# A two-layer decoder trunk: weight pieces of the next projection set between the transpose groups of the attention turn, and the value products moved to a transpose bank

## The chip, the core and the metric

The kernel runs on one core of a Trainium2 chip. The metric is the device time of one execution in microseconds, and the times below are medians over the runs of the kernel before.

## The reference

Two layers of a decoder trunk work on 512 tokens of width 2048 in float32. The first layer is a mixer of gated recurrence and spatial gating with one input and one output projection; the change doesn't touch it. The second layer is multi-head latent attention with 16 heads, and the change lies in it:

```
z = h @ w_in
cq, ckv, kpe, gate = split_sizes(z, [C_Q_RANK, C_KV_RANK, C_ROPE, C_WIDTH])
q = (rms_norm(cq, q_norm) @ w_qb).reshape(bsz, T, C_HEADS, C_QK)
kv = (rms_norm(ckv, kv_norm) @ w_kvb).reshape(bsz, T, C_HEADS, C_NOPE + C_V)
...
s = jnp.einsum('bqhd,bkhd->bhqk', q_blk.astype(jnp.float32), kf) * scale
s = jnp.where(k_idx[None, :] <= q_idx[:, None], s, neg)
p = jax.nn.softmax(s, axis=-1)
return jnp.einsum('bhqk,bkhv->bqhv', p.astype(v.dtype), v)
...
return (o * jax.nn.silu(gate)) @ w_out
```

Ranks are 512, a head has 128 plain and 64 rotary query columns (C_QK is 192) and 128 value columns.

## The kernel before

Each float32 factor of a projection is split into a high and a low part that TensorE takes at full rate, and each product is three matmuls (high x high, high x low, low x high). `feat_steps` (L214 to L216) has the weights as the stationary operand, `tok_steps` (L209 to L211) the activations. Weights come as a plan of pieces of 128 x 1024 or fewer elements. `piece(n)` hands out piece n and starts the load of the pieces up to n + 3: a DMA into a ring of three `raw` tiles, a cast to `whi` on ScalarE (L168, or L177 for a piece cut in two column sets) and a subtraction to `wlo` on VectorE (L169, L178), in rings of four. `split_into` (L279 on ScalarE, L280 on VectorE) makes the two parts of any other tile, and so empties a PSUM bank.

The eight PSUM banks are three rings: `mm` of four, `sc` of two, `tp` of two. A tile that is asked for takes the place of the oldest of its ring, whose readers must be done.

The attention goes by pairs of heads. For pair p there are `proj_q` (36 matmuls in two pieces into three banks, then the rotation L761 to L765 and the splits), `proj_k` (24 matmuls into two banks) and `proj_v` (24 matmuls of 256 columns for each of two banks). A turn of head h is made of four functions. `att_transpose(h)` turns the probabilities of h in three groups (L900: four, four and two 128 x 128 transposes, each into a `tp` bank, each split into PT tiles). `att_scores(h + 1)` makes the scores of the next head by 20 matmuls (L878 to L882) into two `sc` banks and one `mm` bank, and then its softmax: causal mask and row maximum (L885), its negative (L888), the exponential on ScalarE (L889), reciprocal and scaling (L891, L892), in row blocks 3, 2, 0, 1. `att_values(h)` multiplies values by probabilities (L911 to L913, 12 matmuls) into a third `sc` tile, which L914 multiplies by the gate. Below, **turn A** is the turn of an even head, which runs beside the query projection of the next pair, and **turn B** that of an odd head, beside its key and value projections.

The functions are written in this order, and a scheduler then places each instruction in the queue of its engine by priority and estimated readiness; each queue runs in order. So the order on an engine can differ from the order of the calls: in turn A the third transpose group stands among the scores, and the value products stand behind the first matmuls of `proj_k`.

Of the kernel before, what the change touches and what calls it, by code (L numbers as in the profile page):

```python
# [10 lines left out]
F32 = mybir.dt.float32  # L11
# [7 lines left out]
P = 128  # L19
# [25 lines left out]
def trunk_kernel(ctx, tc, x, positions, norm_pre, norm_post, ev_w_in, ev_lb_logits, ev_a_onorm,  # L45
                 ev_b_ln_w, ev_b_ln_b, ev_b_ws, ev_b_bias, ev_w_out, od_w_in, od_q_norm, od_w_qb,
                 od_kv_norm, od_w_kvb, od_w_out, inv_freq, out, x1_dram):
    nc = tc.nc
# [3 lines left out]
    sm = ctx.enter_context(tc.tile_pool(name="sm", bufs=2))  # L52
# [4 lines left out]
    def mm_bank():  # L57
        return pmm.tile([P, 512], F32, name="mm", tag="mm")

    def sc_bank():  # L60
        return psc.tile([P, 512], F32, name="sc", tag="sc")

    def tp_bank():
        return ptp.tile([P, 512], F32, name="tp", tag="tp")
# [123 lines left out]
    def piece(n):  # L188
        issue_to(n + AHEAD)
        return ready.pop(n)  # L190
# [16 lines left out]
    def tok_steps(o, act, k, sl, wh, wl, first, last):  # L207
        hh, hl = act(k)
        nc.tensor.matmul(o, hh[:, sl], wh, start=first, stop=False, skip_group_check=True)  # L209
        nc.tensor.matmul(o, hh[:, sl], wl, start=False, stop=False, skip_group_check=True)  # L210
        nc.tensor.matmul(o, hl[:, sl], wh, start=False, stop=last, skip_group_check=True)  # L211

    def feat_steps(ps, hi, lo, hh, hl, first, last):
        nc.tensor.matmul(ps, hi, hh, start=first, stop=False)  # L214
        nc.tensor.matmul(ps, hi, hl, start=False, stop=False)  # L215
        nc.tensor.matmul(ps, lo, hh, start=False, stop=last)  # L216
# [61 lines left out]
    def split_into(dst_hi, dst_lo, src):  # L278
        nc.scalar.copy(dst_hi, src)  # L279
        nc.vector.tensor_tensor(dst_lo, src, dst_hi.bitcast(F32), ALU.subtract)  # L280
# [35 lines left out]
    pl = {}  # L316
# [440 lines left out]
    cq_act, ckv_act = c_act(0), c_act(8)  # L757
# [11 lines left out]
    stk, _ = piece(pl["kpe"])  # L769
# [37 lines left out]
    def q_of(h):  # L807
        u = 12 * ((h // 2) % 2) + 2 * (h % 2)
        return R[:, u, :], R[:, u + 1, :]

    def k_of(h):
        u = 12 * ((h // 2) % 2) + 4 + 2 * (h % 2)
        return R[:, u, :], R[:, u + 1, :]

    def v_of(p):
        u = 12 * (p % 2) + 8
        return (R[:, u:u + 2, :].rearrange("p a (i c) -> p (a i) c", c=256),
                R[:, u + 2:u + 4, :].rearrange("p a (i c) -> p (a i) c", c=256))

    def p_of(h):  # L820
        base = 3 * (h % 2)
        pb = G[:, base + 1, :]
        return {3: G[:, base, :], 2: pb[:, 0:384], 0: pb[:, 384:512], 1: G[:, base + 2, 0:256]}

    def proj_q(p):
        qps = [mm_bank() for _ in range(3)]
        for s in range(2):
            wh, wl = piece(pl["q", p] + s)
            for t in (2, 0, 1):
                ts = slice(t * P, (t + 1) * P)  # L830
                for kk in range(2):
                    k = 2 * s + kk
                    hh, hl = cq_act(k)
                    feat_steps(qps[t], wh[:, kk, ts], wl[:, kk, ts], hh, hl, k == 0, k == 3)
        rope_half(zr, qps[2], qps[2], sw, 128)
        for m in range(2):
            split_into(*q_of(2 * p + m), qps[m])
            own, oth = slice(64 * m, 64 * m + 64), slice(64 - 64 * m, 128 - 64 * m)
            qs_ = QS[(2 * p + m) % 4]
            nc.scalar.copy(qs_[own], zr[own])  # L840
            nc.vector.tensor_tensor(qs_[oth], zr[own], qs_[own].bitcast(F32), ALU.subtract)  # L841
# [3 lines left out]
    def proj_k(p):  # L845
        kps = [mm_bank() for _ in range(2)]
        kv_pieces[p] = [piece(pl["kv", p] + s) for s in range(2)]
        for m in range(2):
            ms = slice(m * 256, m * 256 + 128)
            for k in range(4):  # L850
                wh, wl = (w[:, k % 2] for w in kv_pieces[p][k // 2])
                hh, hl = ckv_act(k)
                feat_steps(kps[m], wh[:, ms], wl[:, ms], hh, hl, k == 0, k == 3)
            split_into(*k_of(2 * p + m), kps[m])

    def proj_v(p, a):
        Vh, Vl = v_of(p)
        vps = mm_bank()
        for i in range(2):
            sl = slice((2 * a + i) * P, (2 * a + i + 1) * P)  # L860
            for k in range(4):
                wh, wl = (w[:, k % 2].rearrange("p (a c) -> p a c", a=2)[:, :, 128:256]
                          for w in kv_pieces[p][k // 2])
                tok_steps(vps[:, i * 256:i * 256 + 256], ckv_act, k, sl, wh, wl, k == 0 and i == 0, k == 3)
        split_into(Vh[:, 2 * a:2 * a + 2, :].rearrange("p i c -> p (i c)"),
                   Vl[:, 2 * a:2 * a + 2, :].rearrange("p i c -> p (i c)"), vps)

    def att_scores(h):
        (Qh, Ql), (Kh, Kl), qs_, pv = q_of(h), k_of(h), QS[h % 4], p_of(h)
        mx = sm.tile([P, 4], F32, name="mx")  # L870
        nm = sm.tile([P, 4], F32, name="nm")
        su = sm.tile([P, 4], F32, name="su")
        sa, sb, sc = sc_bank(), sc_bank(), mm_bank()
        sp = {3: sa, 2: sb[:, 0:384], 0: sb[:, 384:512], 1: sc[:, 0:256]}
        for j in (3, 2, 0, 1):
            n, o = (j + 1) * P, sp[j]
            qs = slice(j * P, (j + 1) * P)
            nc.tensor.matmul(o, Qh[:, qs], Kh[:, 0:n], start=True, stop=False)  # L878
            nc.tensor.matmul(o, Qh[:, qs], Kl[:, 0:n], start=False, stop=False)
            nc.tensor.matmul(o, Ql[:, qs], Kh[:, 0:n], start=False, stop=False)  # L880
            nc.tensor.matmul(o, qs_[:, qs], KS1[:, 0:n], start=False, stop=False)
            nc.tensor.matmul(o, qs_[:, qs], KS2[:, 0:n], start=False, stop=True)  # L882
        for j in (3, 2, 0, 1):
            n = (j + 1) * P
            nc.vector.tensor_tensor_reduce(out=sp[j], in0=sp[j], in1=tri[:, 512 - n:512], scale=1.0,  # L885
                                           scalar=-3e38, op0=ALU.add, op1=ALU.max,
                                           accum_out=mx[:, j:j + 1])
            nc.vector.tensor_scalar(nm[:, j:j + 1], mx[:, j:j + 1], -C_SCALE, None, ALU.mult)  # L888
            nc.scalar.activation(pv[j], sp[j], AF.Exp, bias=nm[:, j:j + 1], scale=C_SCALE,  # L889
                                 accum_out=su[:, j:j + 1])  # L890
            nc.vector.reciprocal(su[:, j:j + 1], su[:, j:j + 1])  # L891
            nc.vector.tensor_scalar(pv[j], pv[j], su[:, j:j + 1], None, ALU.mult)  # L892

    def att_transpose(h):
        pv = p_of(h)
        groups = [[(j, 0) for j in range(4)], [(1, 1), (2, 1), (3, 1), (3, 3)], [(2, 2), (3, 2)]]
        for (ph, pl), grp in zip(PT, groups):
            tp = tp_bank()
            for s, (j, i) in enumerate(grp):
                nc.tensor.transpose(tp[:, s * P:(s + 1) * P], pv[j][:, i * P:(i + 1) * P], ident)  # L900
            split_into(ph, pl, tp[:, 0:len(grp) * P])

    def att_values(h):
        Vh, Vl = v_of(h // 2)
        ops = sc_bank()
        src = [(PT[0], 0, 512), (PT[1], 0, 384), (PT[2], 0, 256), (PT[1], 384, 128)]
        vs = slice((h % 2) * P, (h % 2 + 1) * P)
        for i in range(4):
            (ph, pl), o, n = src[i]
            dst = ops[:, i * P:512]  # L910
            nc.tensor.matmul(dst, Vh[:, i, vs], ph[:, o:o + n], start=(i == 0), stop=False, skip_group_check=True)  # L911
            nc.tensor.matmul(dst, Vh[:, i, vs], pl[:, o:o + n], start=False, stop=False, skip_group_check=True)  # L912
            nc.tensor.matmul(dst, Vl[:, i, vs], ph[:, o:o + n], start=False, stop=(i == 3), skip_group_check=True)  # L913
        nc.vector.tensor_tensor(B[:, h, :], ops, B[:, h, :], ALU.mult)  # L914

    proj_q(0)
    proj_k(0)
    proj_v(0, 0)
    proj_v(0, 1)
    att_scores(0)  # L920
    for p in range(7):
        proj_q(p + 1)
        att_transpose(2 * p)
        att_scores(2 * p + 1)
        att_values(2 * p)
        proj_k(p + 1)
        proj_v(p + 1, 0)
        proj_v(p + 1, 1)
        att_transpose(2 * p + 1)
        att_scores(2 * p + 2)  # L930
        att_values(2 * p + 1)
    att_transpose(14)
    att_scores(15)
    att_values(14)

    def last_head(q):
        if q == 0:
            att_transpose(15)
        if q == 1:
            att_values(15)  # L940

    Wf = new_w("Wf")

# [37 lines left out]
```

## Time and profile before

| | |
|---|---|
| median of 3 runs (lowest, highest) | 1615.24 us (1614.42, 1615.65) |
| the profiled execution, and its span | 1614.67 us, 1613.0 us |
| TensorE busy, share of the span | 1578.8 us, 98% |
| VectorE, ScalarE, GpSimd busy | 754.8, 536.2, 97.1 us |
| mean granted TensorE clock | 0.998 |
| the stretch that holds the attention loop, from the first scores to just past the last value product | 1177.9 to 1442.0 us of the span, 264.1 us |
| one pair of heads, from a value product of turn A to the next (1231.23 to 1264.89) | 33.66 us |

In a row of the timeline stand the start, the duration, the engine, the line of the program, the operation and its tiles; in brackets how long the engine was idle before it, and what ended that. The durations of matmuls that follow each other overlap, since one starts while the one before it drains: what a matmul of a dense stream costs is the distance between two starts. In the view of waits stand, for each line, the total, the number of times and the longest wait.

### The profile page before, as it was taken

To read this page: it belongs to the slowest core of one execution; us is meant where nothing else is said; L and a number is where in the kernel's file an instruction comes from. 1 tells how busy PE (TensorE), PEld (TensorE's weight loads), DVE (VectorE), ACT (ScalarE), POOL (GpSimd) and SP (SyncE) were. 2 spreads that over 40 slices of the span, in tenths; PEclk is the share of its full clock that TensorE was granted. 3 is DMA by queue.
4 is the path that set the end of the run, shared out by engine and by line. 5 is a ranking of instruction groups with operands and counts; after the bars stand their busy time and mean duration, and the time that the engine had idled before them with its cause. 6 is when DMAs were issued, how large, how long until landed. Compare 5 with 4: busy or idle time off the path is not lost. (4 is left out here: it accounts for less than half of the span.)

```text
span 1613.0 us, 20781 instructions
## 1 busy us (share of the span) xinstructions
PE 1578.8 (98%) x8417; PEld 1356.2 (84%) x8417; DVE 754.8 (47%) x1346; ACT 536.2 (33%) x928; POOL 97.1 (6%) x145
## 2 busy tenths in 40 slices
PE   6999999999999999999999999999999999999997
PEld 5888888898888888888899988888888888888887
DVE  7653455535444324442227534223367676662234
ACT  6422222222222212332225433222355555542221
POOL 1000000000023004000001000000000000000000
PEclk9999999999999999999999999999999999999999
DMA  7322222223333332333326423333311211232224
GB/s 220 118 88 79 91 92 79 92 81 96 92 99 118 99 103 93 127 115 109 100 92 203 125 79 92 93 103 92 92 56 56 66 53 60 92 105 99 97 92 157
DMA packets 124299, 161.03 MB, mean 100 GB/s; under 512 B 7830, under 2 KB 86696, under 8 KB 124200
## 3 DMA queue, kind: packets, MB, share of 16 engines
q1 hardware_dynamic: 124204, 159.71, 31.7%
q8 instruction: 66, 1.08, 0.3%
q14 instruction: 29, 0.24, 0.0%
HBM read 151.30 MB, written 8.39 MB: 99 GB/s over the span
## 5 line engine op out<-in xcount | busy, mean ns | idle before, releaser
L169 DVE TENSOR_TENSOR wlo<-raw,whi 128x1024 fp32r<-128x1024 f32 x240 | 297.2, 1239 | 637.8 <-ACT whi L168 618.1
L168 ACT CAST whi<-raw 128x1024 fp32r<-128x1024 f32 x240 | 252.4, 1053 | 771.7 <-PE mm L211 341.1
L209 PE MATMUL mm<-whi,R 128*128 128x512 f32 (+1 forms) x1152 | 397.0, 345 | 0.5 <-ACT whi L168 0.5
L210 PE MATMUL mm<-wlo,R 128*128 128x512 f32 (+1 forms) x1152 | 395.1, 343 | 1.1 <-DVE wlo L169 1.1
L211 PE MATMUL mm<-whi,R 128*128 128x512 f32 (+1 forms) x1152 | 395.2, 343 | 0.0
L214 PE MATMUL mm<-R,whi 128*128 128x512 f32 x832 | 326.0, 392 | 0.0
L216 PE MATMUL mm<-R,wlo 128*128 128x512 f32 x832 | 324.0, 389 | 0.0
L215 PE MATMUL mm<-R,whi 128*128 128x512 f32 x832 | 323.9, 389 | 0.0
L210 PEld LDWEIGHTS mm<-wlo,R 128*128 128x128 f32 x1152 | 218.6, 190 | 26.1 <-DVE wlo L169 1.6
L209 PEld LDWEIGHTS mm<-whi,R 128*128 128x128 f32 x1152 | 218.5, 190 | 25.6 <-ACT whi L168 0.7
L211 PEld LDWEIGHTS mm<-whi,R 128*128 128x128 f32 x1152 | 218.5, 190 | 25.1
L216 PEld LDWEIGHTS mm<-R,wlo 128*128 128x128 f32 x832 | 156.2, 188 | 32.7
L214 PEld LDWEIGHTS mm<-R,whi 128*128 128x128 f32 x832 | 156.2, 188 | 32.1
L215 PEld LDWEIGHTS mm<-R,whi 128*128 128x128 f32 x832 | 156.3, 188 | 31.9
L214 PE MATMUL mm<-Wc,whi 128*128 128x512 f32 x160 | 62.8, 393 | 0.0
L215 PE MATMUL mm<-Wc,whi 128*128 128x512 f32 x160 | 62.7, 392 | 0.0
L216 PE MATMUL mm<-Wc,wlo 128*128 128x512 f32 x160 | 62.5, 390 | 0.0
L280 DVE TENSOR_TENSOR R<-mm,R 128x512 fp32r<-128x512 f32 x48 | 33.1, 689 | 31.4 <-ACT R L279 31.1
L280 DVE TENSOR_TENSOR R<-tp,R 128x512 fp32r<-128x512 f32 x64 | 42.7, 686 | 2.5 <-ACT R L279 1.9
L279 ACT CAST R<-tp 128x512 fp32r<-128x512 f32 x64 | 36.1, 592 | 17.1 <-PE tp L297 16.0
L279 ACT CAST R<-mm 128x512 fp32r<-128x512 f32 x48 | 28.1, 586 | 38.0 <-PE mm L216 19.5
L889 ACT ACTIVATE G<-sc,nm 128x512 f32<-128x512 f32 (+2 forms) x48 | 26.1, 545 | 35.2 <-DVE nm L888 35.1
(245 smaller groups left out, 1657.1 us busy)
## 6 DMA issues: line engine op xcount, KB each, us to landing
raw<-in_ev_w_in_dram SPq DMA_DIRECT2D x112, 512.0 KB, 3.6
raw<-in_od_w_in_dram SPq DMA_DIRECT2D x49, 512.0 KB, 3.7
raw<-in_ev_w_out_dram SPq DMA_DIRECT2D x32, 512.0 KB, 3.6
raw<-in_od_w_out_dram SPq DMA_DIRECT2D x32, 512.0 KB, 3.6
raw<-in_od_w_kvb_dram SPq DMA_DIRECT2D x16, 512.0 KB, 3.5
raw<-in_od_w_qb_dram SPq DMA_DIRECT2D x16, 384.0 KB, 3.3
Wa<-in_x_dram SPq DMA_DIRECT2D x16, 256.0 KB, 6.3
G<-in_x_dram SPq DMA_DIRECT2D x16, 256.0 KB, 5.0
```

Source lines behind the costliest of these rows:

```text
L168: nc.scalar.copy(hi[:, 0:n], raw[:, 0:n])
L169: nc.vector.tensor_tensor(lo[:, 0:n], raw[:, 0:n], hi[:, 0:n].bitcast(F32), ALU.subtract)
L209: nc.tensor.matmul(o, hh[:, sl], wh, start=first, stop=False, skip_group_check=True)
L210: nc.tensor.matmul(o, hh[:, sl], wl, start=False, stop=False, skip_group_check=True)
L211: nc.tensor.matmul(o, hl[:, sl], wh, start=False, stop=last, skip_group_check=True)
L214: nc.tensor.matmul(ps, hi, hh, start=first, stop=False)
L215: nc.tensor.matmul(ps, hi, hl, start=False, stop=False)
L216: nc.tensor.matmul(ps, lo, hh, start=False, stop=last)
L279: nc.scalar.copy(dst_hi, src)
L280: nc.vector.tensor_tensor(dst_lo, src, dst_hi.bitcast(F32), ALU.subtract)
L889: nc.scalar.activation(pv[j], sp[j], AF.Exp, bias=nm[:, j:j + 1], scale=C_SCALE, accum_out=su[:, j:j + 1])
```

## The change

Four things are altered in the attention loop.

`proj_q` is called for one piece at a time, and its rotation and splits become `evac_q`, called after the scores; `proj_v` and its split are parted likewise. `att_transpose` takes a flag and makes either the first two groups or the third. In turn A the first piece of the next `proj_q` (18 matmuls) stands ahead of groups one and two, and the second piece (18) between them and group three; in turn B the second half of `proj_v` (24) stands between them. So every group is followed by a piece of projection work before its split parts are used.

`att_scores` loses its softmax, which becomes `att_softmax` and is called behind the value products.

`att_values` takes its bank from the ring `tp` instead of `sc`, runs its four column groups in the order 0, 1, 3, 2, so that the group which reads the third transpose group comes last, and its multiplication by the gate becomes `att_gate`.

The last pair runs through the same loop without projections.

```diff
+    qbanks = {}
+
+    def proj_q(p, s):
+        if s == 0:
+            qbanks[p] = [mm_bank() for _ in range(3)]
+        qps = qbanks[p]
+        wh, wl = piece(pl["q", p] + s)
+        for t in (2, 0, 1):
...
+    def evac_q(p):
+        qps = qbanks.pop(p)
         rope_half(zr, qps[2], qps[2], sw, 128)
         for m in range(2):
             split_into(*q_of(2 * p + m), qps[m])
...
+        soft[h] = sp
+
+    def att_softmax(h):
+        sp, pv = soft.pop(h), p_of(h)
...
-    def att_transpose(h):
+    def att_transpose(h, last):
         pv = p_of(h)
         groups = [[(j, 0) for j in range(4)], [(1, 1), (2, 1), (3, 1), (3, 3)], [(2, 2), (3, 2)]]
-        for (ph, pl), grp in zip(PT, groups):
+        for (ph, pl), grp in (zip(PT[2:], groups[2:]) if last else zip(PT[:2], groups[:2])):
             tp = tp_bank()
...
-        ops = sc_bank()
+        ops = tp_bank()
...
-        for i in range(4):
+        for i in (0, 1, 3, 2):
...
-            nc.tensor.matmul(dst, Vl[:, i, vs], ph[:, o:o + n], start=False, stop=(i == 3), skip_group_check=True)
+            nc.tensor.matmul(dst, Vl[:, i, vs], ph[:, o:o + n], start=False, stop=(i == 2), skip_group_check=True)
+        return ops
+
+    def att_gate(h, ops):
         nc.vector.tensor_tensor(B[:, h, :], ops, B[:, h, :], ALU.mult)
...
-    for p in range(7):
-        proj_q(p + 1)
-        att_transpose(2 * p)
-        att_scores(2 * p + 1)
-        att_values(2 * p)
-        proj_k(p + 1)
-        proj_v(p + 1, 0)
-        proj_v(p + 1, 1)
-        att_transpose(2 * p + 1)
-        att_scores(2 * p + 2)
-        att_values(2 * p + 1)
...
+    att_softmax(0)
+    for p in range(8):
+        h = 2 * p
+        if p < 7:
+            proj_q(p + 1, 0)
+        att_transpose(h, False)
+        if p < 7:
+            proj_q(p + 1, 1)
+        att_transpose(h, True)
+        att_scores(h + 1)
+        if p < 7:
+            evac_q(p + 1)
+        ops = att_values(h)
+        att_softmax(h + 1)
+        att_gate(h, ops)
+        if p < 7:
+            proj_k(p + 1)
+            evac_v(p + 1, 0, proj_v(p + 1, 0))
+            att_transpose(h + 1, False)
+            vps = proj_v(p + 1, 1)
+            att_transpose(h + 1, True)
+            evac_v(p + 1, 1, vps)
+            att_scores(h + 2)
+            ops = att_values(h + 1)
+            att_softmax(h + 2)
+            att_gate(h + 1, ops)
```

In the changed kernel the scores stand on L886 to L890, the softmax on L900 to L907, the transposes on L915, the value products on L926 to L928 and the gate on L932.

On TensorE, around the third transpose group of turn A of a steady pair, before (`sc` are score banks, `tp` transpose banks, G holds the probabilities):

```order
L879 MATMUL sc<-R 128x384
L880 MATMUL sc<-R 128x384
L881 MATMUL sc<-KS,R 128x384
L900 MATMUL tp<-ident,G 128x128 x2
L882 MATMUL sc<-KS,R 128x384
L878 MATMUL sc<-R 128x128
L879 MATMUL sc<-R 128x128
L880 MATMUL sc<-R 128x128
```

And now, the same group in the same turn:

```order
L214 MATMUL mm<-Wc,whi 128x512
L215 MATMUL mm<-Wc,whi 128x512
L216 MATMUL mm<-Wc,wlo 128x512
L915 MATMUL tp<-ident,G 128x128 x2
L886 MATMUL sc<-R 128x512
L887 MATMUL sc<-R 128x512
```

Before, nine score matmuls stood between the first two groups and the third; now the 18 matmuls of the second piece do, and all the scores follow.

On TensorE, around the start of the value products of turn A, before (mm_8925 is the first bank of the key projection):

```order
L214 MATMUL mm_8925<-Wc_6332,whi_8783 128x512
L215 MATMUL mm_8925<-Wc_6332,whi_8783 128x512
L216 MATMUL mm_8925<-Wc_6332,wlo_8784 128x512
L214 MATMUL mm_8925<-Wc_6332,whi_8783 128x512
L911 MATMUL sc_8911<-R_76 128x512
L912 MATMUL sc_8911<-R_76 128x512
```

And now (mm_8852 is the score bank of row block 1):

```order
L887 MATMUL mm_8852<-R_76 128x256
L888 MATMUL mm_8852<-R_76 128x256
L889 MATMUL mm_8852<-KS_6333,R_76 128x256
L890 MATMUL mm_8852<-KS_6333,R_76 128x256
L926 MATMUL tp_8888<-R_76 128x512
L927 MATMUL tp_8888<-R_76 128x512
```

The value products have moved from behind the first ten key matmuls to right behind the scores, and write a `tp` tile.

On VectorE, in turn B, from the split of the last value bank to the first negated maximum of the softmax, before (PT is the third transpose group's tile, mx and nm are the row maximum and its negative):

```order
L169 TENSOR_TENSOR wlo<-raw,whi 128x1024
L280 TENSOR_TENSOR R<-mm,R 128x512
L280 TENSOR_TENSOR R<-tp,R 128x512 x2
L885 ISA sc,mx<-sc,G 128x512
L885 ISA mx 128x1
L280 TENSOR_TENSOR PT_79<-tp,PT_79 128x256
```

And now:

```order
L280 TENSOR_TENSOR R<-tp,R 128x512 x2
L169 TENSOR_TENSOR wlo<-raw,whi 128x1024
L280 TENSOR_TENSOR PT_79<-tp,PT_79 128x256
L280 TENSOR_TENSOR R<-mm,R 128x512
L900 ISA sc,mx<-sc,G 128x512
L900 ISA mx 128x1
L169 TENSOR_TENSOR wlo<-raw,whi 128x1024
L903 TENSOR_SCALAR nm<-mx 128x1
```

The splits of the first two groups have moved ahead of the weight piece's subtraction and of the last value split, and a second weight piece's subtraction now stands between the first row maximum and its negative; before, it stood behind the first scaling.

More of the change, by code (lines that the diff above doesn't have):

```diff
@@ L823, in p_of @@
         return {3: G[:, base, :], 2: pb[:, 0:384], 0: pb[:, 384:512], 1: G[:, base + 2, 0:256]}
[L825 to L834, printed above, removed]
+    qbanks = {}
[5 more added lines that the diff above has]
+        for t in (2, 0, 1):
+            ts = slice(t * P, (t + 1) * P)
+            for kk in range(2):
+                k = 2 * s + kk
+                hh, hl = cq_act(k)
+                feat_steps(qps[t], wh[:, kk, ts], wl[:, kk, ts], hh, hl, k == 0, k == 3)
+    def evac_q(p):
+        qps = qbanks.pop(p)
         rope_half(zr, qps[2], qps[2], sw, 128)
@@ L856, in proj_v @@
     def proj_v(p, a):
-        Vh, Vl = v_of(p)
         vps = mm_bank()
@@ L864, in proj_v, with evac_v @@
                 tok_steps(vps[:, i * 256:i * 256 + 256], ckv_act, k, sl, wh, wl, k == 0 and i == 0, k == 3)
+        return vps
+    def evac_v(p, a, vps):
+        Vh, Vl = v_of(p)
         split_into(Vh[:, 2 * a:2 * a + 2, :].rearrange("p i c -> p (i c)"),
                    Vl[:, 2 * a:2 * a + 2, :].rearrange("p i c -> p (i c)"), vps)
+    soft = {}
     def att_scores(h):
[L869 to L872, printed above, removed]
+        (Qh, Ql), (Kh, Kl), qs_ = q_of(h), k_of(h), QS[h % 4]
         sa, sb, sc = sc_bank(), sc_bank(), mm_bank()
@@ L882, in att_scores @@
             nc.tensor.matmul(o, qs_[:, qs], KS2[:, 0:n], start=False, stop=True)
+        soft[h] = sp
+    def att_softmax(h):
+        sp, pv = soft.pop(h), p_of(h)
+        mx = sm.tile([P, 4], F32, name="mx")
+        nm = sm.tile([P, 4], F32, name="nm")
+        su = sm.tile([P, 4], F32, name="su")
         for j in (3, 2, 0, 1):
@@ L912, in att_values @@
             nc.tensor.matmul(dst, Vh[:, i, vs], pl[:, o:o + n], start=False, stop=False, skip_group_check=True)
-            nc.tensor.matmul(dst, Vl[:, i, vs], ph[:, o:o + n], start=False, stop=(i == 3), skip_group_check=True)
+            nc.tensor.matmul(dst, Vl[:, i, vs], ph[:, o:o + n], start=False, stop=(i == 2), skip_group_check=True)
+        return ops
+    def att_gate(h, ops):
         nc.vector.tensor_tensor(B[:, h, :], ops, B[:, h, :], ALU.mult)
-    proj_q(0)
+    proj_q(0, 0)
+    proj_q(0, 1)
+    evac_q(0)
     proj_k(0)
-    proj_v(0, 0)
-    proj_v(0, 1)
+    for a in range(2):
+        evac_v(0, a, proj_v(0, a))
     att_scores(0)
-    for p in range(7):
-        proj_q(p + 1)
-        att_transpose(2 * p)
-        att_scores(2 * p + 1)
-        att_values(2 * p)
-        proj_k(p + 1)
-        proj_v(p + 1, 0)
-        proj_v(p + 1, 1)
-        att_transpose(2 * p + 1)
-        att_scores(2 * p + 2)
-        att_values(2 * p + 1)
-    att_transpose(14)
-    att_scores(15)
-    att_values(14)
+    att_softmax(0)
[24 more added lines that the diff above has]
+            att_gate(h + 1, ops)
     def last_head(q):
         if q == 0:
-            att_transpose(15)
+            att_transpose(15, False)
+            att_transpose(15, True)
         if q == 1:
-            att_values(15)
+            att_gate(15, att_values(15))
     Wf = new_w("Wf")
```

## The prediction

> **What bounds the kernel now.** I read the page first, then the waits of TensorE, then the stages, then TensorE's timeline around each wait.
>
> ```profile
> PE 1578.8 (98%) x8417; PEld 1356.2 (84%) x8417; DVE 754.8 (47%) x1346; ACT 536.2 (33%) x928; POOL 97.1 (6%) x145
> PE tp L297 <- DVE B L292: 14.3, 7, 11.0
> PE sc L911 <- ACT G L889: 4.4, 12, 0.5
> PE tp L900 <- DVE R L280: 3.6, 7, 1.3
> 1177.90:1442.00 264.10, 256.04 (x1496) 222.21 (x1495) 183.12 (x515) 146.41 (x322) 9.00 (x7) 1.00 0.22 71
> ```
>
> TensorE is the bound: it is busy 98% of the span, and the change neither adds nor takes away a matmul. So only its gaps can be won. The 14.3 us on L297 lie in the first layer, out of reach. In the attention stretch 264.10 - 256.04 = 8.1 us are idle, and two lines hold it all: 4.4 us before the value products (L911), 3.6 us before the third transpose group (L900). The clock in this row is 1.00, so there is no throttle to win back.
>
> An idle gap is not the whole loss, since matmuls of a dense stream overlap. The timeline shows both kinds of wait, and a start of the value products without one:
>
> ```profile
> 1226.06 0.33 PE L881 MATMUL sc<-KS,R 128*128 128x384 f32 x1
> 1226.72 0.44 PE L900 MATMUL tp<-ident,G 128*128 128x128 f32 x2 [0.33 <-DVE R L280]
> ...
> 1230.40 0.39 PE L214 MATMUL mm<-Wc,whi 128*128 128x512 f32 x1
> 1231.23 0.50 PE L911 MATMUL sc<-R 128*128 128x512 f32 x1 [0.45 <-ACT G L889]
> 1231.57 0.40 PE L912 MATMUL sc<-R 128*128 128x512 f32 x1
> ...
> 1233.19 0.45 PE L215 MATMUL mm<-Wc,whi 128*128 128x512 f32 x1
> ...
> 1246.55 0.40 PE L214 MATMUL mm<-Wc,whi 128*128 128x512 f32 x1
> 1247.01 0.39 PE L216 MATMUL mm<-Wc,wlo 128*128 128x512 f32 x1
> 1247.64 0.50 PE L911 MATMUL sc<-R 128*128 128x512 f32 x1 [0.25 <-ACT G L889]
> 1247.98 0.40 PE L912 MATMUL sc<-R 128*128 128x512 f32 x1
> ...
> 1400.09 0.39 PE L911 MATMUL sc<-R 128*128 128x512 f32 x1
> 1400.31 0.39 PE L912 MATMUL sc<-R 128*128 128x512 f32 x1
> ...
> 1424.32 0.50 PE L911 MATMUL sc<-R 128*128 128x512 f32 x1 [0.42 <-ACT G L889]
> ```
>
> Two 512-column matmuls in a row (1246.55 to 1247.01) start 0.23 us apart. In turn A the value products start 0.83 us after the matmul before them, 0.60 too late, and their second matmul comes 0.34 behind the first, 0.11 too late: 0.71 us lost, with 0.45 of it idle. In turn B it is 0.40 + 0.11 = 0.51 us, with 0.25 idle. So each such wait loses its idle time and 0.26 us more, for draining and refilling. At 1400.09 the products did not wait, and lost nothing. The transpose at 1226.72 starts 0.66 us after a 384-column matmul, which takes three quarters of 0.23, or 0.17: 0.49 lost, its idle 0.33 and 0.16 more.
>
> Why they wait:
>
> ```profile
> 1230.40 0.69 ACT L889 ACTIVATE G<-sc,nm 128x512 f32<-128x512 f32 x1 [2.58 <-DVE nm L888]
> 1230.99 0.19 ACT L889 ACTIVATION_READ_ACCUMULATOR G<-sc,nm 128x1 f32 x1
> ```
>
> The products take a third tile of a ring of two `sc` banks, so they wait until the exponential of row block 3 of the next head has read the first one (1231.18 here; they start at 1231.23). The third transpose group takes the first group's `tp` bank, which VectorE's split has not emptied when only nine score matmuls stand between.
>
> **The change, part by part.**
>
> *Value products in a `tp` bank, behind the scores.* The wait for the exponential goes. Of the 12, one belongs to the last pair, and I count it with the tail: 1424.32, 0.42 idle. The other 11 lose 4.4 - 0.4 + 11 x 0.26 = 6.8 us. What is next late is their own bank: it is that of the second transpose group, and the last column group reads the third group's split. In turn A that group stands 18 matmuls (4.1 us) after groups one and two, and the scores stand between it and the products:
>
> ```profile
> 1181.25 0.40 PE L214 MATMUL mm<-Wc,whi 128*128 128x512 f32 x1
> ...
> 1189.44 1.03 PE L900 MATMUL tp<-ident,G 128*128 128x128 f32 x8
> ...
> 1236.44 0.28 PE L209 MATMUL mm<-whi,Wc 128*128 128x256 f32 x1
> ...
> 1242.20 1.03 PE L900 MATMUL tp<-ident,G 128*128 128x128 f32 x8
> 1242.99 0.48 PE L878 MATMUL sc<-R 128*128 128x512 f32 x1
> ```
>
> 36 query matmuls take 8.19 us (1181.25 to 1189.44), 18 take 4.1; 48 value-projection matmuls take 5.76 (1236.44 to 1242.20), 24 take 2.9. Eight transposes take 0.79, two 0.2, and a set of scores 3.2 us: from 1242.99 to 1246.55 with two transposes and their hand-over (0.4) in it. Until the products' last column group there are thus 3.2 us of scores and 1.5 of products. In them ScalarE and VectorE must split one 128 x 256 tile, behind one or two other pieces of at most 1.2 us each: about 2 us to spare.
>
> *Third group behind a projection piece.* All seven waits go: 3.6 + 7 x 0.16 = 4.7 us. Cover: 4.1 us in turn A, 2.9 in turn B, against a split of the first group of
>
> ```profile
> L280 DVE TENSOR_TENSOR R<-tp,R 128x512 fp32r<-128x512 f32 x64 | 42.7, 686 | 2.5 <-ACT R L279 1.9
> L279 ACT CAST R<-tp 128x512 fp32r<-128x512 f32 x64 | 36.1, 592 | 17.1 <-PE tp L297 16.0
> ```
>
> 0.59 + 0.69 us, plus on VectorE one split or a weight piece of 1.1 ahead of it: 2.5 us at most.
>
> *Groups one and two sooner after the softmax.* This is the new risk. In a steady turn A they stood behind 36 matmuls and now behind 18. From the end of a set of scores, TensorE now has the value products (1233.19 - 1231.23 - 0.11 = 1.85 us) and 4.1 of query projection: 5.95 us until it needs all four blocks of probabilities. The softmax in this new order, a weight piece's subtraction between first maximum and negative, exists already in the first turn:
>
> ```profile
> 1180.40 0.69 DVE L885 CUSTOM_DVE_ANT_0 sc<-sc,G 128x512 f32<-128x512 f32 x1
> ...
> 1181.01 1.22 DVE L169 TENSOR_TENSOR wlo<-raw,whi 128x1024 fp32r<-128x1024 f32 x1
> 1182.14 0.15 DVE L888 TENSOR_SCALAR nm<-mx 128x1 f32<-128x1 f32 x1
> ...
> 1184.89 0.35 DVE L892 TENSOR_SCALAR G<-G,su 128x256 f32<-128x256 f32 x1
> ...
> 1186.03 0.69 DVE L178 TENSOR_TENSOR wlo<-raw,whi 128x512 fp32r<-128x512 f32 x1 [0.78 <-ACT whi L177]
> ...
> 1187.03 0.28 DVE L892 TENSOR_SCALAR G<-G,su 128x128 f32<-128x128 f32 x1
> ...
> 1250.10 0.68 DVE L914 TENSOR_TENSOR B<-sc,B 128x512 f32<-128x512 f32 x1
> 1250.75 0.53 DVE L892 TENSOR_SCALAR G<-G,su 128x256 f32<-128x256 f32 x2
> ```
>
> Scores end at 1181.25, and block 1 is scaled by 1185.24, 4.0 us later. The steady turn adds the gate product (0.6) and block 0 (0.3): 4.9 us, 1 us before TensorE asks. Before, with the weight piece behind the first scaling, it was 1251.28 - 1246.55 = 4.7 us. So no wait in the steady pairs. In the first pair block 0 stood behind a weight cast and was done at 1187.31; there the scheduler put 26 matmuls ahead of the group (1181.25 + 26 x 0.2275 = 1187.17), so it waits about 0.15 idle: 0.3 us with its 0.16. In turn B 24 key and 24 value matmuls (5.5 + 2.9) stand in between, far more than is needed.
>
> *Later rotation and splits.* `evac_q` now stands behind the scores in the program, and its three `mm` banks are held longer. The first key bank takes the place of the first query bank.
>
> ```profile
> L761 ACT COPY G<-mm 32x512 f32<-32x512 f32 x16 | 9.3, 579 | 5.5 <-PE mm L216 5.4
> L762 ACT COPY G<-mm 32x512 f32<-32x512 f32 x16 | 9.2, 577 | 0.2
> ```
>
> TensorE comes to it 0.2 + 3.2 + 1.85 = 5.25 us after the second piece; four such copies (2.3 us) and one split (0.59 + 0.69) come to 3.6, and the copies start while the piece runs. No wait.
>
> *The tail.* Now the first two groups of head 14 stand close behind its scores, and the scores of head 15 wait for a bank. Before, the tail loses 0.68 at 1424.32 and about half a microsecond in short hand-overs. Now VectorE has splits for the output projection in that softmax. I count a wait of 0.6 for the second score bank and 0.5 for the third group, which has no piece between: an estimate from the durations above. Net zero, with 0.8 us either way.
>
> *Sum.* 6.8 + 4.7 - 0.3 + 0 = 11.2 us. The profiled execution, 1614.67 us, becomes 1603.5; the median, 0.57 above it, 1604.0.
>
> **The rule that speaks against the size.** The refill is read from the weight load:
>
> ```profile
> 1231.23 0.19 PEld L911 LDWEIGHTS sc<-R 128*128 128x128 f32 x1 [0.87 <-ACT G L889]
> ```
>
> It starts together with the delayed matmul, though its weights had long been there. The Trainium skill ("TensorE: Matmul & The Clock Gate", Part 2) says that the queue pulls weight loads ahead of running matmuls. By that alone a wait would lose its idle time only, and the sum would be 4.0 + 3.6 - 0.3 = 7.3 us. The trace does not agree for a load that itself holds the wait.
>
> **The rivals.**
>
> *Only the idle time comes back.* The 0.26 and 0.16 stay at each hand-over, because the products now follow another group of matmuls whose semaphores are late. For it: every start behind a wait shows it. Against it: 1400.09. Gain 7.3 us, 1607.9 us. Chance 0.10.
>
> *Groups one and two wait in turn A.* If the weight cast of the first turn stands ahead of block 0 in every pair, the softmax takes 1187.31 - 1181.25 + 0.6 = 6.7 us, 0.75 more than the cover; with 0.16 each, six pairs lose 5.5. Gain 5.7, 1609.5 us. The order of the changed kernel speaks against it: there the cast stands behind the softmax. Chance 0.09.
>
> *The value products still wait*, now for the split of the third group. Gain only 4.7 - 0.3 = 4.4, 1610.8 us. Against it the 2 us to spare. Chance 0.04.
>
> *Slower.* The weight piece's subtraction stands on VectorE ahead of the negated maximum, so if its data land late the whole softmax does, and groups one and two with it. One such wait is in the trace, in the tail:
>
> ```profile
> DVE wlo L169 <- DMA G<-x_dram: 3.4, 1, 3.4
> ```
>
> With 3.4 us in each of six pairs the softmax takes 8.3 us, 2.35 over the cover; with 0.16, six pairs lose 15.1, and the sum is 11.2 - 15.1: 1619.1 us. It decides against the kernel from a delay of about 3.3 us per pair. Against it: no attention piece waits for a transfer now. Chance 0.03.
>
> *No difference.* The waits come back elsewhere on TensorE with nearly the old sum. Chance 0.03.
>
> **How the numbers follow.** The forecast has 0.71. A difference of 0.2%, 3.2 us, is about what a measurement of this kernel can tell from none. Faster takes the forecast and the first three rivals, 0.94; same 0.03, slower 0.03. The range goes down to 1601.5: the whole tail (1.2 us) and the first pair's 0.3 won as well give 12.7 us, 1602.5, and 1 us for the spread of the runs. Up it goes past the second rival, to 1610.
>
> **What would show it.** Right: the waits of TensorE no longer show L926 in the loop, and L915 only in the first pair and the tail; a value product starts 0.23 us or less after the last score; a pair takes 33.66 - 0.71 - 0.51 - 0.49 = 31.95 us. Wrong: a wait of L915 on VectorE's scaling (L907) in each turn A, or a wait of L926 on L280.

## The result, and the profile after

The changed kernel takes 1602.34 us (median of 5 runs, 1602.01 to 1602.72), the kernel before in the same session 1615.57. The ratio is 0.9923, 95% interval 0.9912 to 0.9934: 12.4 us less, with 10.7 to 14.2 as the interval (the two medians alone are 13.2 apart). The profiled execution took 1602.72 us with a span of 1601.0, 12.0 us under the span before. The forecast was 1604.0 and 11.2 us.

The changed kernel's page, its waits of TensorE and the stretch of the attention loop (its columns: the stretch and its length, busy time and count of TensorE, of its weight loads, of VectorE, ScalarE and GpSimd, then clock, DMA share and GB/s):

```profile
PE 1574.7 (98%) x8417; PEld 1359.2 (85%) x8417; DVE 752.5 (47%) x1346; ACT 534.6 (33%) x928; POOL 96.6 (6%) x145
```

```profile
PE tp L297 <- DVE B L292: 14.6, 6, 12.1
...
PE sc L886 <- ACT G L904: 0.3, 1, 0.3
```

```profile
1177.90:1442.00 264.10, 263.66 (x1555) 234.52 (x1554) 183.90 (x517) 147.26 (x324) 9.11 (x7) 1.00 0.24 74
```

In the attention loop neither the value products (now L926) nor the transposes (now L915) wait any longer; one wait is left, 0.3 us ahead of the scores of the last head (L886). In the same 264.1 us TensorE is now busy 263.66 instead of 256.04, and 59 more matmuls fit in. The wait of the first layer is as it was (14.6 us, before 14.3).

The timeline of TensorE in a steady pair shows the two places:

```profile
1226.72 0.28 PE L890 MATMUL mm<-KS,R 128*128 128x256 f32 x1
1226.84 0.40 PE L926 MATMUL tp<-R 128*128 128x512 f32 x1
1227.07 0.40 PE L927 MATMUL tp<-R 128*128 128x512 f32 x1
...
1255.02 0.39 PE L216 MATMUL mm<-Wc,wlo 128*128 128x512 f32 x1
1255.25 0.38 PE L915 MATMUL tp<-ident,G 128*128 128x128 f32 x2
1255.39 0.48 PE L886 MATMUL sc<-R 128*128 128x512 f32 x1
...
1258.91 0.40 PE L927 MATMUL tp<-R 128*128 128x512 f32 x1
...
1386.24 0.40 PE L927 MATMUL tp<-R 128*128 128x512 f32 x1
```

The first value product follows the last score by 0.12 us and the second by 0.23; the third group follows its projection piece by 0.23. Neither starts late. From 1227.07 to 1258.91 a pair takes 31.84 us, and five pairs to 1386.24 take 159.17, 31.83 each, where it was 33.66.

VectorE's softmax in turn B, and the transposes of turn A that need it:

```profile
1243.46 0.69 DVE L900 CUSTOM_DVE_ANT_0 sc<-sc,G 128x512 f32<-128x512 f32 x1
...
1244.07 1.22 DVE L169 TENSOR_TENSOR wlo<-raw,whi 128x1024 fp32r<-128x1024 f32 x1
1245.21 0.14 DVE L903 TENSOR_SCALAR nm<-mx 128x1 f32<-128x1 f32 x1
...
1247.21 0.16 DVE L906 RECIPROCAL su<-su 128x1 f32<-128x1 f32 x1 [0.33 <-ACT G L904]
...
1248.62 0.53 DVE L907 TENSOR_SCALAR G<-G,su 128x256 f32<-128x256 f32 x2
...
1250.02 0.39 PE L216 MATMUL mm<-Wc,wlo 128*128 128x512 f32 x1
1250.25 1.04 PE L915 MATMUL tp<-ident,G 128*128 128x128 f32 x8
```

The weight piece's subtraction stands between the first maximum and its negative, as the prediction had it. The probabilities are ready at 1249.15 and TensorE comes to them at 1250.25: 1.1 us to spare, 1.0 predicted.

### The profile page after: what moved, and what is told of

It is laid out like the page before. It is cut to its first block, busy times and chain, and to the rows that moved or that the text cites. A ratio compares the mean times of both kernels' runs of the same rounds, so it can differ in the third digit from the quotient of the medians.

```text
span 1601.0 us, 20791 instructions
## 1 busy us (share of the span) xinstructions
PE 1574.7 (98%) x8417; PEld 1359.2 (85%) x8417; DVE 752.5 (47%) x1346; ACT 534.6 (33%) x928; POOL 96.6 (6%) x145
## 5 line engine op out<-in xcount | busy, mean ns | idle before, releaser
L280 DVE TENSOR_TENSOR R<-mm,R 128x512 fp32r<-128x512 f32 x48 | 32.9, 686 | 27.5 <-ACT R L279 27.5
L280 DVE TENSOR_TENSOR R<-tp,R 128x512 fp32r<-128x512 f32 x64 | 42.1, 684 | 4.0 <-ACT R L279 3.7
```

## The experiments

The theory was that the value products' waits (6.8 us) and the third group's (4.7) go, each worth its idle time and a refill. Three things had to be told apart: whether the two terms are independent, whether the idle time or more is won, and how much the softmax has to spare. Three switches make up the change: the **bank** of the value tile (`tp` or `sc`), the **piece** between the transpose groups, and the **later place** of the query banks' emptying, of the last value bank's split and of the softmax. Runs of all eight settings stand in this table; the column order 0, 1, 3, 2, which goes with the later place, is tested by itself below. The kernel before has a median of 1614.57 to 1614.68 in the sessions of the other runs; the changed kernel was timed in the session of the result, where it has 1615.57, so differences to the changed kernel are good to about 1 us by the medians alone.

| bank | piece | later place | label | median, us | ratio to before, interval | span, us |
|---|---|---|---|---|---|---|
| - | - | - | before | 1614.66 | 1 | 1613.0 |
| - | - | yes | later_emptying_only | 1614.95 | 1.0003 (0.9994, 1.0012) | 1613.2 |
| - | yes | - | piece_only | 1615.93 | 1.0008 (0.9999, 1.0017) | 1613.7 |
| - | yes | yes | v_back_in_sc | 1615.61 | 1.0007 (0.9998, 1.0016) | 1613.8 |
| yes | - | - | v_bank_only | 1611.51 | 0.9980 (0.9971, 0.9988) | 1609.6 |
| yes | - | yes | groups_together | 1606.09 | 0.9948 (0.9935, 0.9960) | 1604.4 |
| yes | yes | - | both_old_program_order | 1603.12 | 0.9929 (0.9915, 0.9942) | 1600.6 |
| yes | yes | yes | the changed kernel | 1602.34 | 0.9923 (0.9912, 0.9934) | 1601.0 |

Without the bank, nothing else moves the time by as much as 1.5 us. With it, either of the other two brings most of the rest.

### The bank alone

```diff
-        ops = sc_bank()
+        ops = tp_bank()
```

> Kernel before with one line changed: the value products take their tile from the tp ring; order of groups, softmax and projections as before. My theory: the 11 waits of the loop for the exponential go, each worth its idle time and 0.26 us more: 6.8 us less than before, about 1608.8, while the wait of the third transpose group (7 times, 0.33 to 0.5 us idle, on the split of the first group) stays as it was. Rival, only idle time comes back: 4.0 us less, 1611.6. Rival, the products now wait for the split of the third group, which stands only 9 to 11 score matmuls ahead of them: 0 to 3 us less, with waits of the value line on VectorE.

Measured: 3.1 us less than before by the medians, less than half of my 6.8. The waits of TensorE in the attention turns, and the place in turn A on VectorE and TensorE:

```profile
PE tp L900 <- DVE R L280: 3.6, 7, 1.3
PE tp L911 <- DVE R L280: 2.9, 6, 0.5
```

```profile
1225.76 0.68 DVE L280 TENSOR_TENSOR R<-tp,R 128x512 fp32r<-128x512 f32 x1
1226.47 1.41 DVE L841 TENSOR_TENSOR R<-G,R 64x512 fp32r<-64x512 f32 x2
1227.90 0.69 DVE L280 TENSOR_TENSOR R<-tp,R 128x512 fp32r<-128x512 f32 x1
```

```profile
1227.97 0.28 PE L882 MATMUL mm<-KS,R 128*128 128x256 f32 x1
1228.74 0.47 PE L911 MATMUL tp<-R 128*128 128x512 f32 x1 [0.49 <-DVE R L280]
```

The wait for the exponential is gone. The products now stand right behind the scores, where the scheduler had put ten key matmuls ahead of them before, and in turn A another wait has taken the old one's place: the products' own bank is that of the second transpose group, and VectorE empties it only at 1228.59, since the rotation's subtractions (L841) stand between its splits of the first and the second group. The third rival was right that the products would wait for VectorE, and wrong about which split: it is the second group's. The wait of the third group stayed, 3.6 us.

### The piece alone

The loop of before with the transposes moved:

```diff
-        proj_q(p + 1)
-        att_transpose(2 * p)
+        proj_q(p + 1, lambda: att_transpose(2 * p, (0, 2)))
+        att_transpose(2 * p, (2, 3))
...
         proj_v(p + 1, 0)
+        att_transpose(2 * p + 1, (0, 2))
         proj_v(p + 1, 1)
-        att_transpose(2 * p + 1)
+        att_transpose(2 * p + 1, (2, 3))
```

> Kernel before with the transposes alone moved: groups one and two stand behind the first projection piece, group three behind the second; the value tile stays in the sc ring. If the two terms are independent, as my sum took them: 4.7 us less than before, 1610.9. My theory after reading the changed kernel's trace: the value products still wait for the exponential of row block 3, whose end is set from the end of those scores by VectorE and ScalarE, and TensorE now has only the rest of the scores and 8 query matmuls until then (7 in turn B). In turn A exponential 3 ends 5.3 us after the last score matmul of block 3 starts, scores and 8 matmuls are through after 4.1: 1.2 us idle instead of 0.45, so what the third group gives is lost at the products: 0 to 2 us slower than before, 1615.5 to 1617.5, idle before the value products 9 to 11 us in all instead of 4.4, none before the third group.

Measured: 1615.93 us, no gain (ratio 1.0008, 0.9999 to 1.0017), as expected after reading the changed kernel's trace, and 5 us from what independent terms would give. The wait of the third group is gone, and the value products (L913 in this kernel) wait 9.7 us instead of 4.4. The wait, and the place in turn A, with the first and the last of the key matmuls that stand between scores and products:

```profile
PE sc L913 <- ACT G L891: 9.7, 14, 1.4
```

```profile
1228.29 0.40 PE L214 MATMUL mm<-Wc,whi 128*128 128x512 f32 x1
...
1229.91 0.39 PE L215 MATMUL mm<-Wc,whi 128*128 128x512 f32 x1
1230.58 0.69 ACT L891 ACTIVATE G<-sc,nm 128x512 f32<-128x512 f32 x1 [2.44 <-DVE nm L890]
...
1231.41 0.50 PE L913 MATMUL sc<-R 128*128 128x512 f32 x1 [1.12 <-ACT G L891]
```

The first key matmul in the kernel before:

```profile
1228.33 0.40 PE L214 MATMUL mm<-Wc,whi 128*128 128x512 f32 x1
```

So in turn A of the kernel before, two waits stood in series ahead of one event, the exponential of row block 3, and without the first of them TensorE idles 1.12 us at the second instead of 0.45. These 0.67 us have two parts. Counted from the first key matmul, right behind the scores, the products start after 3.12 us here (1228.29 to 1231.41) and after 2.90 before (1228.33 to 1231.23): the exponential comes 0.22 later after the scores, and that is the series. The other 0.46 is the order: the scheduler put 8 key matmuls ahead of the products here and 10 before, so two matmuls of 0.23 us are missing in the gap. The third group's wait was priced at 0.49 us in this turn. With ten key matmuls ahead, 0.27 of it would have been won, by an estimate from these rows; no run here fixes their number, so how much of the missing gain is the series and how much the scheduler's order is not shown by experiment.

### The later place alone

The changed kernel with the value tile in `sc` and the pieces ahead of all groups:

```diff
             proj_q(p + 1, 0)
+            proj_q(p + 1, 1)
         att_transpose(h, False)
-        if p < 7:
-            proj_q(p + 1, 1)
...
-            att_transpose(h + 1, False)
             vps = proj_v(p + 1, 1)
+            att_transpose(h + 1, False)
...
-        ops = tp_bank()
+        ops = sc_bank()
```

> The changed kernel without its two parts: projection pieces ahead of all three groups, value tile in the sc ring. What is left of the change is that the query banks are emptied and the softmax is issued behind the scores (and the column groups' order). It shows what that place is worth where neither part is there; with the value tile in the tp ring it is worth the 5.4 us between the two kernels that have groups together. Theory: the value products wait for the exponential again, and a wait ahead of it on TensorE that goes only lengthens this one; VectorE has the same work before the first maximum, whichever comes first. As the kernel before within 1.5 us, 1613 to 1616, 4 to 7 us idle on the value line. Rival, the later place is a gain of its own: 4 to 6 us less than before, 1609 to 1611.

Measured: 1614.95 us, as before. Both waits are there:

```profile
PE sc L926 <- ACT G L904: 4.1, 8, 0.6
PE tp L915 <- DVE R L280: 2.8, 7, 0.6
```

### The bank undone

One line of the changed kernel, `ops = sc_bank()` again.

> Changed kernel with one line undone: the value tile comes from the sc ring again, the third group stays behind its projection piece. If the terms are independent: 6.8 us more than the changed kernel, about 1609. My theory: exponential 3 ends 5.3 us after the last score matmul of row block 3 starts in turn A, TensorE is there after 4.1, so the seven products of turn A idle 1.2 us each and those of turn B 0.25; with 0.11 to 0.26 more for each wait 11 to 14 us in all, and the whole gain is gone: 1613.5 to 1616.5. If only idle time counts: the difference equals the idle time listed before the value line.

Measured: 13.3 us more than the changed kernel by the medians, 12.8 by the spans; independent terms would have given 6.8. The whole gain is gone. The waits, and the place in turn A (PEld is the weight load):

```profile
PE sc L926 <- ACT G L904: 9.6, 14, 1.4
```

```profile
1230.71 0.69 ACT L904 ACTIVATE G<-sc,nm 128x512 f32<-128x512 f32 x1 [2.43 <-DVE nm L903]
...
1231.54 0.19 PEld L926 LDWEIGHTS sc<-R 128*128 128x128 f32 x1 [1.52 <-ACT G L904]
1231.54 0.50 PE L926 MATMUL sc<-R 128*128 128x512 f32 x1 [1.09 <-ACT G L904]
...
1231.88 0.39 PE L927 MATMUL sc<-R 128*128 128x512 f32 x1
```

Here too 8 key matmuls stand ahead of the products in turn A. The 9.6 us of idle time cost 12.8 us of span, so idle time alone would leave 3.2 us unexplained. The price of one wait is read better from the steady pairs, since the span also holds the first layer, whose longest row of waits goes from 13.5 to 15.1 us over these runs. Four pairs, from the first value product of a turn A, take 134.98 us here (1231.54 to 1366.52), 33.75 each, against 127.33 in the changed kernel (1226.84 to 1354.17), 31.83 each. These 1.91 us hold 1.30 of idle time (1.09 in turn A, 0.21 in turn B), so each of the two waits costs 0.30 us beyond its idle time, where the prediction had 0.26. The load that holds the wait starts with its matmul, as in the kernel before, and the second matmul comes 0.34 behind the first.

### The piece undone

The first two hunks of the later place's diff, with the value tile left in `tp`.

> Changed kernel with the projection pieces of a turn ahead of all three transpose groups again; the value tile stays in the tp ring, softmax and emptying as changed. Theory: the third group waits for the split of the first again, 9 score matmuls apart in turn A (0.33 us idle and 0.16 more, 7 times: 3.4 us) and only 7 apart in turn B, where in the kernel before the split ended 0.6 us after the seventh score matmul starts: 0.5 to 0.7 us, 7 times; 3.4 to 8.2 us more than the changed kernel, 1606 to 1610.5, and groups one and two of the first pair don't wait. Rival, the third group's wait is hidden behind other waits: under 1 us more. Only idle time counts: the difference equals the idle time of the transposes.

Measured: 1606.09 us, 3.8 more than the changed kernel (3.4 by the spans), at the lower end. TensorE waits at the third group again, in turn A alone, and the value products don't wait:

```profile
PE tp L915 <- DVE R L280: 2.8, 7, 0.7
```

```profile
1225.10 1.28 DVE L280 TENSOR_TENSOR R<-tp,R 128x512 fp32r<-128x512 f32 x2
1226.41 0.69 DVE L847 TENSOR_TENSOR R<-G,R 64x512 fp32r<-64x512 f32 x1
1227.13 0.42 DVE L280 TENSOR_TENSOR PT<-tp,PT 128x256 fp32r<-128x256 f32 x1
```

```profile
1225.84 0.44 PE L915 MATMUL tp<-ident,G 128*128 128x128 f32 x2 [0.31 <-DVE R L280]
...
1227.44 0.40 PE L926 MATMUL tp<-R 128*128 128x512 f32 x1
```

The waits that I had expected in turn B did not come. Against the bank alone this kernel has the later place, and the rows show what that does: both group splits now stand together (L280, x2) ahead of the rotation's subtractions (L847), so the products' bank is empty at 1226.38, 1.06 us before they start. That accounts for the 5.4 us between these two kernels: 2.9 us idle and, at the prediction's price of 0.26, six refills at the products, and 0.8 us less idle at the third group, 5.3 in all.

### Both parts without the later place

> Kernel before with both parts, the value tile in the tp ring and the third group behind the second piece, but with softmax and the emptying of the query banks left where the program of before has them. My theory: these two parts are the whole change, so as the changed kernel within 1 us, 1601.5 to 1603.5. Rival: the later place of the query banks' emptying and of the softmax is part of the gain (VectorE reaches the first maximum sooner or later): over 1.5 us away from it, with other waits in the attention turns.

Measured: 1603.12 us (ratio 0.9929), span 1600.6, by which it can't be told from the changed kernel. With the piece between the groups, the splits of the first two groups are done before the rotation begins, so the products' bank is empty in time. Its trace shows a small loss all the same. In the last turn A that has a projection beside it, VectorE splits the third group only behind the rotation's subtractions, and the products (L914 is one of their lines here) wait for that split:

```profile
PE tp L914 <- DVE PT L280: 0.8, 1, 0.8
```

From the first score to the last value product this trace takes 248.55 us (1177.60 to 1426.15) and that of the changed kernel 247.17 (1179.02 to 1426.19), 1.4 less. The spans hide it, since the first scores start 1.4 us sooner here, though the program ahead of them is the same.

### The softmax's spare time

First from the side of TensorE: groups one and two of turn A stand behind 10 query matmuls in five pairs (14 in the last) instead of 18.

```diff
-        if p < 7:
-            proj_q(p + 1, 0)
         att_transpose(h, False)
         if p < 7:
+            proj_q(p + 1, 0)
             proj_q(p + 1, 1)
```

> Changed kernel with groups one and two of turn A 8 query matmuls (1.8 us) earlier, behind 10 instead of 18 of them, in five pairs (14 in the last, as before in the first). Theory: in the changed kernel the probabilities are ready 1.1 us before TensorE comes to them, so five waits of 0.7 us idle on VectorE's scaling, each with 0.16 more: 4 to 5 us more than the changed kernel, 1606 to 1607.5. Only idle time: 3.5 us more. Rival, the softmax follows TensorE and is not what is spare there: no difference.

Measured: 1607.02 us, 4.7 more by the medians and 4.3 by the spans, as the theory has it:

```profile
PE tp L915 <- DVE G L907: 3.9, 6, 0.7
```

TensorE came 1.8 us sooner and waited 0.7: the difference, 1.1, is the spare time read from the trace.

Then from the side of VectorE, with multiplications by one in each softmax:

```diff
             nc.vector.tensor_scalar(pv[j], pv[j], su[:, j:j + 1], None, ALU.mult)
+            if j == 3:
+                for _ in range(6):
+                    nc.vector.tensor_scalar(pv[j], pv[j], 1.0, None, ALU.mult)
```

> Changed kernel with six more multiplications by one of the 128 x 512 block 3 in each softmax, in place on VectorE, 0.40 to 0.48 us each: the softmax ends 2.1 to 2.5 us later. Theory: 1.1 us of that is spare in turn B's softmax, so groups one and two of turn A wait 1.0 to 1.4 us in six pairs, with 0.16 each 7 to 9 us; turn A's softmax has over 3 us to spare and costs nothing; the tail 1 to 2 us: 8 to 11 us more than the changed kernel, 1610 to 1613. Rival, no spare time: all of it is lost, 14 times 2.4, 34 us. Rival, VectorE's work is far off the path: under 2 us.

Measured: 1607.85 us, 5.5 more, where I had expected 8 to 11; a loss of the whole added time, 34 us, and a loss under 2 us are both excluded. The waits, and rows of VectorE and TensorE in a steady pair (L910 is the added line, L918 the transposes):

```profile
PE tp L918 <- DVE G L907: 3.8, 7, 0.6
...
PE tp L918 <- DVE R L280: 0.4, 1, 0.4
```

```profile
1247.34 0.49 DVE L907 TENSOR_SCALAR G<-G,su 128x512 f32<-128x512 f32 x1
1247.86 0.43 DVE L910 TENSOR_SCALAR G<-G 128x512 f32<-128x512 f32 x1
...
1248.48 0.42 DVE L910 TENSOR_SCALAR G<-G 128x512 f32<-128x512 f32 x1
1248.81 0.41 DVE L907 TENSOR_SCALAR G<-G,su 128x384 f32<-128x384 f32 x1
```

```profile
1251.96 1.06 PE L918 MATMUL tp<-ident,G 128*128 128x128 f32 x8 [0.60 <-DVE G L907]
```

I had priced an added multiplication by its duration, but the next one starts 0.33 us after it. Six are 2.0 us. The first fills the slot in which VectorE was idle for 0.33 us in the changed kernel (1247.21), so the softmax ends some 1.7 later; less the 1.1 to spare, that is 0.6, the wait in the row.

> Changed kernel with two more multiplications by one of block 3 in each softmax (six gave 0.60 us idle in each turn A, and stood 0.33 us apart). Theory: 2 x 0.33 = 0.7 us, part of it in VectorE's idle slots, against 1.1 us to spare: no wait of groups one and two in the steady pairs, the changed kernel's time within 1 us, 1601.5 to 1603.5. Rival, the loss grows in proportion to the work: a third of what six cost, 1.8 us more, 1604.2.

Measured: 1602.38 us (ratio 0.9923, 0.9909 to 0.9936), nothing lost. One wait, not one for each pair, is left on the transposes:

```profile
PE tp L918 <- DVE G L907: 0.2, 1, 0.2
```

Two cost nothing and six cost 5.5: the loss has a threshold, as spare time has, and is not in proportion to VectorE's work.

### The order of the column groups

```diff
-        for i in (0, 1, 3, 2):
+        for i in range(4):
```

> Changed kernel with the products' column groups in the order 0, 1, 2, 3 again, so the third group's split is asked for 0.2 us sooner. Theory: the split has 2 us to spare, so no difference: 1601.5 to 1603.5, no wait on the value line. Rival, it is needed: waits on the value line for the split of the third group, 2 us or more.

Measured: 1602.10 us (ratio 0.9920, 0.9906 to 0.9933), and no row for the value line among the waits. This edit does nothing here.

## Why the prediction was right, and where it was not

**TensorE is the bound, and only its gaps can be won.** Right: the matmuls are the same 8417, and the stretch went from 8.1 us of idle time to 0.4.

**Both waits go, and what is next late is in time.** Right for this kernel. The value products follow the scores by 0.12 us, the third group follows its piece by 0.23, and a pair takes 31.84 us against the forecast of 31.95.

**The sum of two terms, 6.8 and 4.7.** The total was right, 11.2 against 12.0 by the spans and 12.4 by the ratio; as the worth of each part the two terms were wrong. The bank alone is worth 3.1 us and not 6.8. The piece is worth nothing where the bank is not changed, in part because the scheduler then puts fewer key matmuls ahead of the products, and 1611.51 - 1603.12 = 8.4 us where it is. The sum held because a wait's cost, counted on TensorE's timeline, is right for all waits together when all of them go and nothing takes their place. It does not say what one of them is worth while the next still stands.

**"About 2 us to spare" for the products' own bank.** This step holds only with the piece or with the later place. With the bank alone there was nothing to spare: 2.9 us of waits in six turns A. The rival that had the products wait for a split, which I gave 0.04, is therefore what happens to one part of this change, with the second group's split in place of the third's; with both parts and without the later place it happened once as I had written it, 0.84 us for the third group's split.

**The later place, costed at nothing.** Nearly right in the changed kernel: the medians of 1603.12 without it and 1602.34 with it can't be told apart, and the traces differ by 1.4 us between the first score and the last product. In a kernel with the bank and without the piece it is worth 5.4 us. The prediction named the cover of the three query banks, and not the splits that the rotation delays.

**The refill.** The mechanism was right, and both sizes were a little small. The 0.26 us of a value product's wait was 0.30 in the steady pairs of the run that put these waits back. For the transposes, where the prediction had 0.16, the steady pairs of three runs, each over four pairs of one trace against the 31.83 us of the changed kernel, give this: 0.29 at the third group with the groups together (32.45 us a pair, 0.61 more, 0.32 idle), and at the first two groups 0.20 with less cover (32.72, 0.89 more, 0.69 idle) and 0.18 with six multiplications (32.61, 0.78 more, 0.60 idle). The rival that only idle time returns, 7.3 us, is excluded by the result and by the 1.91 us of a pair for 1.30 of idle time. The Trainium skill ("TensorE: Matmul & The Clock Gate", Part 2) lets the queue pull a weight load ahead of running matmuls when its rows of the array don't conflict or when it goes to the background buffer; the row at 1231.54, where the load holds the wait and starts with its matmul, does not show that.

**Groups one and two after the softmax.** Right: 1.1 us to spare against 1.0, measured from both sides. The first pair's small wait came as 0.2 us late instead of 0.3:

```profile
1187.91 0.39 PE L215 MATMUL mm<-Wc,whi 128*128 128x512 f32 x1
1188.34 0.87 PE L915 MATMUL tp<-ident,G 128*128 128x128 f32 x6
```

These start 0.43 us apart, where a dense stream has 0.23.

**The tail.** Counted at a net of nothing, with a wait of 0.6 us for the second score bank; there it is 0.3 us idle (the L886 row of the waits). The span beat the forecast by 0.8 us, and the attention by more: the first scores start 1.0 us later in the changed kernel's trace (1179.02 against 1178.05), though the change leaves the program ahead of them as it was, and from there to the end of the span the gain is 13.0 us. Of the 1.8 over the forecast the six steady pairs hold 0.7, 0.11 each, which the larger refills cover. Where the rest lies, in the first pair or the tail, is not settled.

**The slower rival**, a weight piece whose data come late ahead of the softmax, did not come, and no run here delays a transfer. What such a delay would cost stays open; the 1.1 us to spare and the runs with added work say only when it would begin to cost.

No kernel here beats the changed one by more than the runs can tell: four, from 1602.10 to 1603.12, can't be told apart by their times, and TensorE has 0.4 us idle left in the stretch.

## What to carry to other kernels

Idle times on the bounding engine added up here only when all of them went; where two waits stand ahead of the same late event, removing the first one lengthens the second, and a scheduler may change the work that stands between them, so ask of each wait what TensorE would meet next. The Trainium skill ("Perfetto Trace Analysis", Identifying Performance Opportunities) says that a gap which repeats can mean too little PSUM for the next tile, and that was so here: the ring of two `sc` banks was the gate in front of everything else, yet opening it alone gave 3.1 of 12.4 us, because the bank that the tile moved to was emptied late. Before crediting one part of a change, run it without the others, and the others without it.

## What the runs showed of the hardware that was not expected

A VectorE multiplication of 128 x 512 float32 that the profile shows as 0.42 us long lets the next instruction start 0.33 us behind it (1248.48 to 1248.81), though the rows overlap. Pricing added VectorE work by its duration made the expectation 8 to 11 us where 5.5 came. And a wait of TensorE cost more beyond its idle time than the rows of the kernel before had shown: 0.30 us instead of 0.26 at the value products, and 0.18 to 0.29 instead of 0.16 at the transposes.
